# A hybrid attention and recurrence layer: down and output products with tokens on the partitions, normalised there and turned back by transposes

## The chip, the cores and the metric

The kernel runs on one NeuronCore of a Trainium2 chip. Its engines are TensorE (PE in the profile; its weight loads are PEld), VectorE (DVE), ScalarE (ACT), GpSimd (POOL) and SyncE (SP), which run their own instruction queues in order and wait for each other by semaphores. The metric is device time of one execution, in microseconds (us); less is better.

## The reference

One decoder layer on x of 512 tokens by 1024 features, all in float32:

```python
f = swiglu(rms_norm(h, ffn1_norm_pre), w_gate, w_up, w_down)      # D_FF = 2816
h = h + 0.5 * rms_norm(f, ffn1_norm_post)
u = rms_norm(h, mix_norm_pre)
q, k, v, xr, yr, gl = split(u @ w_in)                             # 3 x 1536, 2 x 1024, 2 x 1024
attn_d = dilated_attention(q, k, v) @ w_attn_branch               # 3 groups of 4 heads of 128
rec_d = (rg_lru(conv(xr)) * gelu(yr)) @ w_rec_branch
merged = sigmoid(gl[0]) * attn_d + sigmoid(gl[1]) * rec_d
h = h + rms_norm(merged @ w_out, mix_norm_post)
f = swiglu(rms_norm(h, ffn2_norm_pre), ...)                       # as the first, own weights
h = h + 0.5 * rms_norm(f, ffn2_norm_post)
```

with `swiglu(x) = (silu(x @ w_gate) * (x @ w_up)) @ w_down` and `rms_norm(x, g) = x * rsqrt(mean(x * x) + 1e-6) * g`, the mean over the 1024 features of a token.

## The kernel before

Activations lie with features on the 128 partitions and the 512 tokens along the free dimension, as eight tiles of 128 features. Every operand of a large product is split in two parts, a rounded copy and the remainder (`split`, L254: ScalarE copies, VectorE subtracts), and a product is three matrix products of the parts (`mm3`, L267). Weights come as one stream of 1 MB groups through two `raw` buffers (`raw_of`, SP's queue), are split into `w8` (four buffers of 1024 columns) or `w4` (three of 512) tiles, and are the stationary operand of `gemm` (L283); activations are the moving one, 512 or 256 tokens wide.

The gate and up products of most feed-forward tiles, and the query, key and gate products of the mixer, are made two at a time by `seven` (L518): the 2 x 2 blocks of weights (two halves of the features by two outputs) and of activations (features by two halves of 256 tokens) are multiplied with seven block products in place of eight. `w_forms` (L499) sums and splits the weights of one such group, one group ahead; `x_forms` (L420) makes the seven forms of the activations once per stage, with sums on VectorE.

The order of one feed-forward part is written out in `ffn_order` (L46): five tiles of 128 hidden features by plain products (`std`), the others by `seven` (`prod`), and between them the down products of the hidden tiles that are ready, in five parts (`FF_PARTS`), one of eight output tiles m of 128 features at a time, spread over the groups. The down sums stay in `facc`. The last part's down products are `last_product` (L371), which the output product of the mixer also uses: the last four output tiles (all eight in the second feed-forward part) are made 256 tokens wide, each is squared on ScalarE and added on VectorE (`sq_add`), and the sum over features is one product by a matrix of ones (`rstd`, L322), as features lie on partitions. Then `residual` adds to h, `pre_norm` makes the next stage's two parts with the gain alone, and the row of reciprocal roots (`r`, one per token) is multiplied onto the products later (`std_out`, `conv`, `branch`, or as `rcol` in `values`), or before the forms are made (`scaled` in `x_forms`). h is written to DRAM after each stage (`kept_m`, `kept`) and loaded again for the next residual, by POOL's queue.

A tile scheduler orders each engine's instructions by their place in the program and by priorities: weights are fetched 100 places ahead (`AHEAD`), evacuations of `seven` 200 (`EVAC`). TensorE's accumulators are five `acc` and three `aux` banks. The stage stretches that the tables use are, from the timeline: feed-forward 1 to 355, values to 423, attention and its gates to 621, attention branch and recurrence to about 833, output product to 890, feed-forward 2 to the end.

Of the kernel before, what the change touches and what calls it, by code (L numbers as in the profile page):

```python
# [10 lines left out]
F32 = mybir.dt.float32  # L11
# [5 lines left out]
P = 128  # L17
T = 512
# [4 lines left out]
NSTD = 5  # L23
NEARLY = 4
# [11 lines left out]
QKB = 7  # L36
CB = 7
# [8 lines left out]
def ffn_order():  # L46

    order = [("std", f) for f in range(NSTD)]  # L50
    order += [("prep", NSTD), ("down", 0, tuple(range(NEARLY)))]
    for a, (f0, f1) in enumerate(FF_PARTS):
        fs = range(max(f0, NSTD), f1)
        m0 = NEARLY if a == 1 else 0
# [9 lines left out]
def down_width(a):  # L64
    return (FF_PARTS[a][1] - FF_PARTS[a][0]) * P


def stream_plan():

    plan = []  # L70

    def ffn(n):
        for ev in ffn_order():
            if ev[0] == "std":
                plan.append((("gate", n, ev[1]), 1024))
                plan.append((("up", n, ev[1]), 1024))
            elif ev[0] == "prep":
                plan.append((("gu", n, ev[1]), 2048))
            else:
                for m in ev[-1]:  # L80
                    plan.append((("down", n, ev[-2], m), down_width(ev[-2])))
        for m in range(KC):
            plan.append((("down", n, len(FF_PARTS) - 1, m), down_width(len(FF_PARTS) - 1)))
# [35 lines left out]
    for m in range(KC):  # L119
        plan.append((("out", m), 1024))  # L120
# [19 lines left out]
for _n, _w in (("g1a", 8), ("g1b", 8), ("gma", 8), ("gmb", 8), ("g2a", 8), ("g2b", 8),  # L140
               ("cw", 32), ("cb", 8), ("bx", 8), ("ba", 8), ("ap", 8)):
    SMALL[_n] = (_o, _w)
    _o += _w
# [5 lines left out]
def hybrid_layer(ctx: ExitStack, tc: tile.TileContext, xT: bass.AP, wst: bass.AP, small: bass.AP,  # L149
                 consts: bass.AP, bias: bass.AP, out: bass.AP):  # L150
# [16 lines left out]
    ghalf = cpool.tile([P, 16], F32, name="ghalf")  # L167
# [9 lines left out]
    def hpair(m, sl):  # L177
        return hs["t"][m // 4][:, m % 4:m % 4 + 2, sl]
# [36 lines left out]
    def fetch(key, slot=None):  # L215

        with tc.high_priority(offset=AHEAD if slot is None else 0):
# [9 lines left out]
    def w4():  # L227
        return wpool.tile([P, 2, 512], F32R, name="w4", tag="w4", bufs=3)
# [60 lines left out]
    def gemm_first(keys, x, slots=None):  # L289
# [3 lines left out]
        for sl in HALVES:  # L293
            for k in range(x.n):
                for wt, ps in zip(wts, pss):
                    mm3(ps[:, sl], k128(wt[0])[:, k, :], k128(wt[1])[:, k, :], x.hi[k][:, sl],
                        x.lo[k][:, sl], k == 0, k == x.n - 1)
        return pss
# [11 lines left out]
    def sq_add(acc, src, sl, first, apart=False):  # L310

        for s in halves(sl):
            if first:
                ACT.activation(acc[:, s], src(s), AF.Square)
            else:
                q = ntile("sq", 2)
                ACT.activation(q, src(s), AF.Square)
                if apart:
                    return q
                DVE.tensor_add(acc[:, s], acc[:, s], q)  # L320

    def rstd(acc, r, sl, extra=None):  # L322
        for s in halves(sl):
            ps = aux_ps()[:, :HB]
            PE.matmul(ps, ones, acc[:, s], start=True, stop=extra is None)
            if extra is not None:
                PE.matmul(ps, ones, extra, start=False, stop=True)
            v, y = ntile("v", 2), ntile("y", 2)
            ACT.activation(y, ps, AF.Abs_reciprocal_sqrt, bias=eps, scale=1.0 / D)
            DVE.scalar_tensor_tensor(v, ps, D * EPS, y, op0=ALU.add, op1=ALU.mult)  # L330
            DVE.scalar_tensor_tensor(v, v, -0.5 / D, y, op0=ALU.mult, op1=ALU.mult)
            DVE.scalar_tensor_tensor(r[:, s], v, 1.5, y, op0=ALU.add, op1=ALU.mult)
# [12 lines left out]
    def pre_rstd(acc, r, sl):  # L345
        for m in range(KC):
            sq_add(acc, lambda s: hm(m, s), sl, m == 0)
        rstd(acc, r, sl)

    def gain(gi, m):  # L350
        return ghalf[:, gi * 8 + m:gi * 8 + m + 1] if gi is not None else col("gmb", m)

    def residual_end(rp, sl):

        rq = ntile("rq", 1)
        ACT.activation(rq, rp[:, sl], AF.Copy)
        t = tpool.tile([P, 2, HB], F32, name="res", tag="t")
        nc.gpsimd.tensor_mul(t, facc[:, 6:8, sl], rq[:, None, :].to_broadcast([P, 2, HB]))
        nc.gpsimd.tensor_add(hpair(6, sl), hpair(6, sl), t)
        for m in (0, 2, 4):  # L360
            t = acc_ps().rearrange("q (m t) -> q m t", m=2)
            DVE.tensor_mul(t, facc[:, m:m + 2, sl], rp[:, None, sl].to_broadcast([P, 2, HB]))
            DVE.tensor_add(hpair(m, sl), t, hpair(m, sl))

    def residual(rp, m, sl):

        t = tpool.tile([P, 2, HB], F32, name="res", tag="t")
        DVE.tensor_mul(t, facc[:, m:m + 2, sl], rp[:, None, sl].to_broadcast([P, 2, HB]))
        DVE.tensor_add(hpair(m, sl), hpair(m, sl), t)

    def last_product(key, x, evac, gi, nxt, then, slots, end=False):  # L371


        acc = npool.tile([P, T], F32, name="acc", tag="acc", bufs=2)
        rp = npool.tile([P, T], F32, name="rp", tag="r", bufs=2)
        nl = 8 if end else 4
        tails = {}
        for m in range(KC - nl):
            ps = acc_ps()
            gemm(ps, fetch(key(m)), x)  # L380
            evac(m, ps, FULL)
            sq_add(acc, lambda s: facc[:, m, s], FULL, m == 0)
            ACT.activation(facc[:, m, :], facc[:, m, :], AF.Copy, scale=gain(gi, m))
        if nl < 8:
            warm(acc)
        wts = [fetch(key(m), None if m < 4 else slots.pop(0)) for m in range(KC - nl, KC)]
        for sl in HALVES:
            for m in range(KC - nl, KC):
                ps = acc_ps()[:, :HB]
                gemm(ps, wts[m - KC + nl], x, sl)  # L390
                evac(m, ps, sl)
                last = sq_add(acc, lambda s: facc[:, m, s], sl, m == 0, end and m == KC - 1)
                ACT.activation(facc[:, m, sl], facc[:, m, sl], AF.Copy, scale=gain(gi, m))
                tails[sl.start] = last
                if m == KC - nl and sl.start:
                    rstd(acc, rp, HALVES[0], tails[0])
        for sl in HALVES:
            if sl.start:
                if end:
                    rp = acc_ps()  # L400
                rstd(acc, rp, sl, tails[HB])
            if end and sl.start:
                residual_end(rp, sl)
            for m in range(KC):
                if m % 2 == 0 and not (end and sl.start):
                    residual(rp, m, sl)
                nxt(sl, m)
        if then:
            for sl in HALVES:
                then(sl)  # L410
# [791 lines left out]
```

## Time and profile before

| | us |
|---|---|
| median of 3 runs (lowest, highest) | 1257.12 (1255.87, 1258.87) |
| the profiled execution | 1255.59 |
| its span, first to last instruction | 1253.8 |
| TensorE busy | 1237.8 |
| VectorE busy | 965.2 |
| ScalarE busy | 706.0 |
| moved by DMA, whole span | 135.67 MB |

The profile is of one execution. Busy time is time with at least one instruction on the engine; TensorE's products overlap, so it is busy also while it goes slower than it could, and the step from one product's start to the next tells more than the durations. The clock that TensorE was granted is 0.998 of full speed over the span. In the profile's tables a line number is that of the kernel's source; where a helper issues the instruction it is the helper's line.

### The profile page before, as it was taken

Reading aid. Unit: us, or ns where it says so; the run is one execution under the profiler, and the core shown is the slowest. Engines: PE = TensorE matmul, PEld = TensorE weight load, DVE = VectorE, ACT = ScalarE, POOL = GpSimd, SP = SyncE. Lnnn points to the kernel's source line nnn. Section 1 sums busy time; section 2 is a strip of 40 time slices with the busy share of each in tenths; the row PEclk is TensorE's granted clock in tenths of the full one; section 3 lists DMA queues with packets and bytes.
Section 4 is the critical chain, followed back from the end, with each engine's and each line's share of the span. In section 5 each row is a group of like instructions: output and inputs, shape, how many; then the busy total and the mean of one; then the engine's idle time right before and its main releaser. Section 6 shows DMA issues by size and latency. Waiting matters only on the chain.

```text
span 1253.8 us, 19539 instructions
## 1 busy us (share of the span) xinstructions
PE 1237.8 (99%) x7952; PEld 1128.7 (90%) x7952; DVE 965.2 (77%) x1547; ACT 706.0 (56%) x1184; POOL 22.6 (2%) x44
## 2 busy tenths in 40 slices
PE   9999999999999999999999999999999999999996
PEld 7889999999888999999988888889988999999996
DVE  7987777787588788889676987753998777777755
ACT  6555444454565565566636879536655544445543
POOL 0000000000002000000100000000000000000000
PEclk9999999999999999999999999999999999999999
DMA  6223333333515232221442231323222222223232
GB/s 241 70 90 102 106 105 104 105 113 129 207 73 167 89 110 77 75 103 68 135 139 96 77 126 67 135 85 117 101 102 93 93 101 102 101 102 118 102 135 68
DMA packets 26811, 135.67 MB, mean 108 GB/s; under 512 B 3297, under 2 KB 5473, under 8 KB 14561
## 3 DMA queue, kind: packets, MB, share of 16 engines
q1 hardware_dynamic: 24064, 122.88, 28.1%
q0 software_dynamic: 2656, 11.54, 2.7%
q8 instruction: 62, 1.02, 0.3%
q14 instruction: 29, 0.23, 0.1%
HBM read 127.07 MB, written 6.29 MB: 106 GB/s over the span
## 4 chain that ended last, share of the span: by engine, by line
PE 87%; DVE 8%; ACT 2%; DMA 1%; issue 1%; SPq 0%; DVEq 0%
PE acc L269 13%; PE acc L268 13%; PE acc L270 13%; PE acc L527 11%; PE acc L528 11%; PE acc L529 11%; PE aux L529 2%; PE aux L528 2%; PE aux L527 2%; DVE w L256 2%; PE acc L736 1%; PE acc L735 1%; PE acc L734 1%; DMA raw<-in_w 1%; DVE acc L320 1%
## 5 line engine op out<-in xcount | busy, mean ns | idle before, releaser
L256 DVE TENSOR_TENSOR w<-raw,w 128x1024 fp32r<-128x1024 f32 (+2 forms) x307 | 302.0, 989 | 110.0 <-ACT w L255 109.7
L255 ACT ACTIVATE w<-raw 128x1024 fp32r<-128x1024 f32 (+2 forms) x307 | 262.5, 867 | 190.5 <-PE aux L529 55.1
L528 PE MATMUL acc<-big,w 128*128 128x256 f32 x928 | 263.4, 284 | 0.0
L527 PE MATMUL acc<-big,w 128*128 128x256 f32 x928 | 263.3, 284 | 0.0
L529 PE MATMUL acc<-big,w 128*128 128x256 f32 x928 | 263.1, 284 | 0.0
L269 PE MATMUL acc<-act,w 128*128 128x512 f32 (+1 forms) x524 | 191.5, 366 | 1.2 <-DVE act L256 0.8
L270 PE MATMUL acc<-act,w 128*128 128x512 f32 (+1 forms) x524 | 191.2, 365 | 0.8 <-DVE w L256 0.8
L268 PE MATMUL acc<-act,w 128*128 128x512 f32 (+1 forms) x524 | 191.4, 367 | 0.0
L527 PEld LDWEIGHTS acc<-big,w 128*128 128x128 f32 x928 | 177.8, 192 | 1.8 <-ACT c L534 0.4
L528 PEld LDWEIGHTS acc<-big,w 128*128 128x128 f32 x928 | 177.8, 192 | 1.4
L529 PEld LDWEIGHTS acc<-big,w 128*128 128x128 f32 x928 | 177.9, 192 | 0.0
L534 ACT ACTIVATE c<-acc 128x256 f32<-128x256 f32 x166 | 63.4, 382 | 98.5 <-PE acc L529 92.5
L270 PEld LDWEIGHTS acc<-act,w 128*128 128x128 f32 x524 | 98.9, 189 | 17.5 <-DVE w L256 1.7
L269 PEld LDWEIGHTS acc<-act,w 128*128 128x128 f32 x524 | 99.0, 189 | 16.6 <-DVE act L256 1.9
L268 PEld LDWEIGHTS acc<-act,w 128*128 128x128 f32 x524 | 98.8, 189 | 15.8 <-ACT act L341 0.6
L268 PE MATMUL acc<-big,w 128*128 128x512 f32 (+1 forms) x240 | 91.7, 382 | 0.0
L270 PE MATMUL acc<-big,w 128*128 128x512 f32 (+1 forms) x240 | 91.7, 382 | 0.0
L269 PE MATMUL acc<-big,w 128*128 128x512 f32 (+1 forms) x240 | 91.7, 382 | 0.0
L528 PE MATMUL aux<-big,w 128*128 128x256 f32 x272 | 77.0, 283 | 0.0
L529 PE MATMUL aux<-big,w 128*128 128x256 f32 x272 | 77.0, 283 | 0.0
L527 PE MATMUL aux<-big,w 128*128 128x256 f32 x272 | 77.0, 283 | 0.0
L256 DVE TENSOR_TENSOR w<-s,w 128x1024 fp32r<-128x1024 f32 x50 | 61.1, 1221 | 4.9 <-ACT w L255 4.9
(278 smaller groups left out, 2411.4 us busy)
## 6 DMA issues: line engine op xcount, KB each, us to landing
raw<-in_w SPq DMA_DIRECT2D x89, 1024.0 KB, 4.9
raw<-in_w SPq DMA_DIRECT2D x23, 512.0 KB, 3.7
raw<-in_w SPq DMA_DIRECT2D x6, 768.0 KB, 4.2
raw<-in_w SPq DMA_DIRECT2D x16, 256.0 KB, 3.0
raw<-in_w SPq DMA_DIRECT2D x3, 896.0 KB, 4.7
h<-in_x SPq DMA_DIRECT2D x8, 256.0 KB, 5.4
h<-in_x POOLq DMA_DIRECT2D x8, 256.0 KB, 5.3
kept_m<-h POOLq DMA_DIRECT2D x2, 1024.0 KB, 4.5
```

Of the source, the lines that this page charges most:

```text
L255: ACT.activation(dh, src, AF.Copy)
L256: DVE.tensor_sub(dl, src, dh.bitcast(F32))
L268: PE.matmul(ps, wh, xh, start=first, stop=False)
L269: PE.matmul(ps, wh, xl, start=False, stop=False)
L270: PE.matmul(ps, wl, xh, start=False, stop=last)
L320: DVE.tensor_add(acc[:, s], acc[:, s], q)
L527: PE.matmul(ps, wh, xh, start=start and k == 0, stop=False, skip_group_check=True)
L528: PE.matmul(ps, wh, xl, start=False, stop=False, skip_group_check=True)
L529: PE.matmul(ps, wl, xh, start=False, stop=k == 3, skip_group_check=True)
L534: ACT.activation(c, ps, AF.Copy)
L734: PE.matmul(pss[b], um.hi[k][:, bl], wh[:, i, :], start=k == 0, stop=False)
L735: PE.matmul(pss[b], um.hi[k][:, bl], wl[:, i, :], start=False, stop=False)
```

## The change

The down products and the output product exchange their operands: 128 tokens of activations are stationary and 512 columns of weights move, so a result has tokens on the partitions, four blocks b of 128 tokens by two halves of 512 features. `facc` and h take that layout (`fb`, `hb`), x is loaded once more in it (`xN`) for the residual, and the output is written in it. A token's mean square is then a sum along the free dimension: `square` takes it as ScalarE's accumulator, and `root` works on columns of 128 x 1. Gains of the norms are rows that a POOL load repeats on all partitions (`gains`).

`Boundary.block` ends a block of tokens: reciprocal root, residual, copy to DRAM, the root of the new h, and u, the normalised input with its gain. `Boundary.turn` transposes u back to features on partitions and makes the two parts of the next input from it, and a plain copy into `facc`. As u is normalised already, the row `r` falls away after feed-forward 1's input; std_out, values, conv and the gates read their products as they are. The same `u` is kept through attention and recurrence; before, its parts were made a second time after attention.

Of the seven forms, three are now the parts themselves; the mixer uses them in place, feed-forward 2 copies them by six POOL transfers. Down products come in halves of 48 products, through two own weight buffers `wd`, in place of output tiles of 12. Feed-forward 2 makes four tiles by plain products in place of five. Pools of `qk`, `c` and `w4` tiles have one buffer less.

```diff
-NSTD = 5
+NSTD = {1: 5, 2: 4}
@@ ffn_order
-    order += [("prep", NSTD), ("down", 0, tuple(range(NEARLY)))]
+    order += [("prep", NSTD[n]), ("down", 0, 0)]
...
-            n, k = len(fs), KC - m0
-            ms = range(m0 - (-k * i // n), m0 - (-k * (i + 1) // n))
-            order.append(("prod", f, a - 1, tuple(ms)))
+            c, k = len(fs), len(halves)
+            order.append(("prod", f, a - 1, halves[i * k // c:(i + 1) * k // c]))
@@
+    def root(sums, f):
+        with tc.high_priority(offset=EVAC):
+            tot, y, v, r = (stat() for _ in range(4))
+            DVE.tensor_add(tot, sums[0], sums[1])
+            ACT.activation(y, tot, AF.Abs_reciprocal_sqrt, bias=eps, scale=1.0 / D)
+            refine(r, v, y, tot, f)
+        return r
+
+    def square(src):
+        q, t = tmp("sq"), stat()
+        ACT.activation(q, src, AF.Square, accum_out=t)
+        return t
+
+    def tokens(ps, ws, x, b, fill=lambda: None):
+        bl = slice(b * P, (b + 1) * P)
+        for k in range(x.n):
+            wh, wl = (w.rearrange("p (k c) -> p k c", k=2)[:, k % 2, :] for w in ws[k // 2])
+            PE.matmul(ps, x.hi[k][:, bl], wh, start=k == 0, stop=False)
+            PE.matmul(ps, x.hi[k][:, bl], wl, start=False, stop=False)
+            PE.matmul(ps, x.lo[k][:, bl], wh, start=False, stop=k == x.n - 1)
+            if k == x.n // 2 - 1:
+                fill()
...
+    def last_product(key, nk, x, added, grow, slots, block, fills={}):
+        sums = {}
+        warm(eps)
+        for half, fs in enumerate(FHALVES):
+            ws = [fetch(key(half, kk), slots.pop(0) if half else None) for kk in range(nk)]
+            for b in range(4):
+                ps = acc_ps()
+                tokens(ps, ws, x, b, fills.get((half, b), lambda: None))
+                src, y = ps, fb(b, fs)
+                if added:
+                    DVE.tensor_add(y, ps, y)
+                    src = y
+                sums[b, half] = square(src)
+                DVE.tensor_mul(y, src, grow[:, fs])
+                if half:
+                    block(b, (sums[b, 0], sums[b, 1]))
+
+    class Boundary:
...
+        def block(self, b, sums):
+            r = root(sums, self.f)
+            DVE.scalar_tensor_tensor(hb(b), fb(b), r, hb(b), op0=ALU.mult, op1=ALU.add)
+            nc.gpsimd.dma_start(self.kept[b], hb(b))
+            r = root([square(hb(b, fs)) for fs in FHALVES], 1.0)
+            us = []
+            for fs in FHALVES:
+                u = tmp("u")
+                DVE.scalar_tensor_tensor(u, hb(b, fs), r, self.grow[:, fs], op0=ALU.mult, op1=ALU.mult)
+                us.append(u)
+            self.u[b] = us
+
+        def turn(self, b):
+            for i, u in enumerate(self.u.pop(b)):
+                ps = aux_ps()
+                for j in range(4):
+                    PE.transpose(ps[:, j * P:(j + 1) * P], u[:, j * P:(j + 1) * P], ident)
+                src = ps.rearrange("p (k t) -> p k t", k=4)
+                hi, lo = (t[:, :, b * P:(b + 1) * P] for t in (self.his[i], self.los[i]))
+                ACT.activation(hi, src, AF.Copy)
+                DVE.tensor_sub(lo, src, hi.bitcast(F32))
+                ACT.activation(fb(b, FHALVES[i]), ps, AF.Copy)
...
+        def copies():
+            for name in ("p1", "p2", "p3"):
+                v = big([P, 2, 4, HB])
+                for i in range(2):
+                    nc.gpsimd.dma_start(v[:, i], t[name][i])
+                t[name] = v[:, 0], v[:, 1]
...
+    def block1(b, sums):
+        bd1.block(b, sums)
+        if b >= 2:
+            bd1.turn(b - 2)
+
+    last_product(*end1, True, grow1, spare(ap1), block1)
@@ values, first group
-                for bs in ((0, 1), (2, 3)):
+                for b in range(4):
                     for kk in range(4):
-                        part(kk, bs)
-                roots()
+                        part(kk, (b,))
+                    if b < 2:
+                        bd1.turn(b + 2)
...
+    last_product(lambda half, kk: ("out", half, kk), 4, mg, False, grow3, slots, bd2.block,
+                 {(1, 3): lambda: (bd2.turn(0), bd2.turn(1))})
+    keys = [(w, 2, i) for i in range(NSTD[2]) for w in ("gate", "up")]
+    pss = gemm_first(keys[:NFIRST], u2, [spare(ap2)[2]],
+                     {3: [lambda: bd2.turn(2)], 4: [lambda: bd2.turn(3)]})
...
+    def block2(b, sums):
+        r = root(sums, 0.5)
+        for fs in FHALVES:
+            DVE.scalar_tensor_tensor(hb(b, fs), fb(b, fs), r, hb(b, fs), op0=ALU.mult, op1=ALU.add)
+            nc.sync.dma_start(out[b][:, fs], hb(b, fs))
```

More of the change, by code (lines that the diff above doesn't have):

```diff
@@ L365, in residual @@
[L365 to L410, printed above, removed]
@@ L435, in form_t2 @@
-        def form_t2():
-            form("p6", d[2], pool.tile([P, 2, 4, HB], F32R, name="tx", tag="tx"))
+            v = tile_ if tile_ is not None else big([P, 2, 4, HB])
+            t[name] = v[:, 0], v[:, 1]
+            split(v[:, 0], v[:, 1], src)
         def sum1():
```

365 lines of the change are left out of this document (181 added, 184 removed).

## The prediction

> **What bounds the kernel now.** I read the page's busy times and its chain first, then TensorE's timeline in the middle of a feed-forward block, then the stage table, and last the end of VectorE's timeline. The page:
>
> ```profile
> PE 1237.8 (99%) x7952; PEld 1128.7 (90%) x7952; DVE 965.2 (77%) x1547; ACT 706.0 (56%) x1184; POOL 22.6 (2%) x44
> ...
> PE 87%; DVE 8%; ACT 2%; DMA 1%; issue 1%; SPq 0%; DVEq 0%
> ```
>
> TensorE is hardly ever idle and holds 87% of the chain, so the time is a count of matrix products times their spacing, plus what TensorE waits where stages meet, plus head and tail. The spacing is read from start to start, not from the durations, which overlap:
>
> ```profile
> 305.47 0.28 PE L528 MATMUL aux<-big,w 128*128 128x256 f32 x1
> 305.59 0.28 PE L529 MATMUL aux<-big,w 128*128 128x256 f32 x1
> ...
> 305.71 0.40 PE L268 MATMUL acc<-act,w 128*128 128x512 f32 x1
> 305.95 0.40 PE L269 MATMUL acc<-act,w 128*128 128x512 f32 x1
> 306.18 0.39 PE L270 MATMUL acc<-act,w 128*128 128x512 f32 x1
> ```
>
> A product 256 wide takes 0.120 us, one 512 wide 0.227 us (the median over all of them; single steps here read 0.23 and 0.24). The stage table (columns: stretch; length; busy us and records of PE, PEld, DVE, ACT, POOL; clock; DMA) says where the other engines press:
>
> ```profile
> 338.00:424.00 86.00, 85.95 (x450) 73.43 (x450) 70.07 (x116) 50.78 (x90) 8.95 (x18) 1.00 0.34 116
> 665.00:775.00 110.00, 108.78 (x478) 89.10 (x477) 90.94 (x119) 87.97 (x113) 0.00 (x0) 1.00 0.27 96
> 833.00:959.00 126.00, 124.85 (x756) 111.44 (x755) 95.73 (x151) 72.65 (x128) 1.09 (x2) 1.00 0.29 105
> 959.00:1205.00 246.00, 246.00 (x1749) 232.35 (x1748) 185.49 (x281) 123.60 (x202) 1.06 (x2) 1.00 0.33 113
> ```
>
> PE busy hides small waits, so I counted the timeline. From 862.46 to 958.43 (second half of the output product, start of feed-forward 2) there are 444 products 256 wide (53.3 us), 168 of 512 (38.1) and 8 fp32 records of the row sums (0.215 each, 1.7): 93.1 us of work in 95.97, so 2.9 us waited. From 338.05 to 423.46 (end of feed-forward 1, values) the same count leaves 0.6. The tail:
>
> ```profile
> 1241.75 0.42 DVE L618 TENSOR_TENSOR facc<-acc,facc 128x256 f32<-128x256 f32 x1 [0.83 <-PE acc L270]
> 1243.92 0.42 DVE L330 SCALAR_TENSOR_TENSOR v<-aux,y 128x256 f32<-128x256 f32 x1 [1.75 <-ACT y L329]
> 1245.72 1.29 DVE L362 TENSOR_TENSOR acc<-facc,acc 128x512 f32<-128x512 f32 x2 [0.45 <-ACT rq L356]
> 1248.84 0.69 DVE L363 TENSOR_TENSOR h<-acc,h 128x512 f32<-128x512 f32 x1
> ```
>
> The last product's slot ends at 1241.55 and the span at 1253.8: 12.3 us of tail, 4.3 of them after VectorE's last instruction (output transfer and end).
>
> **The change part by part.** The profiled execution took 1255.59 us (span 1253.8), 1.5 under the median of 1257.12; differences are worked on the span and laid on the median.
>
> *TensorE's own work.* (a) 624 products of half width (144 in feed-forward 1's last product, 192 in the output product, 288 in feed-forward 2's) become 312 of full width with activations stationary: 624 x 0.120 = 74.9 against 312 x 0.227 = 70.8, -4.1. That form is in the trace already (values, L734 to L736) at the same 0.227. By the Trainium skill, TensorE: Matmul & The Clock Gate, section Back-to-back issue gap, a warm isolated product takes N/2.4 + 2.5 ns, 109 and 216; (a) would then be worth an estimated 0.8 and the forecast 1252.6. The trace's 120 and 227 disagree with it, so I take the trace and give the rule no chance. (b) Tile 4 of feed-forward 2 goes from two plain products (48 x 0.227 = 10.9) to the seven-product form (84 x 0.120 = 10.1): -0.8. (c) Ten row-sum products by ones before the last product's end, 0.43 each by two records: -4.3; four transposes of roots: -0.4. (d) 64 transposes, at 0.44 per four by the chain's rows of L879: +7.0. Sum -2.6.
>
> *Waits that go.* At 324.7 (0.31) and 1207.4 (0.95) TensorE waits for the last activation tile to be split, with only one or two small down products (2.7 us each) as cover. After, a whole down half (48 x 0.227 = 10.9) stands there: -1.3. What is late next is the first gain row, whose load waits for that half's weight buffer: VectorE waits for it, and TensorE has five accumulators, 20 us at 4.1 us per token block, against 5.3 us for a POOL load. Cost nothing.
>
> *The two boundaries.* The order of the changed kernel as built says what TensorE does meanwhile. After feed-forward 1 each token block ends a chain on VectorE and ScalarE: sum 0.69, square 0.66 plus reading the accumulator 0.1, root 1.09 (one-column instructions at 0.20 start to start as L861 and L862, a reciprocal root at 0.29 as the warm-up on L336), residual over 1024 columns 1.28, two squares 1.32, root 1.09, two gain products 1.35, eight handovers at 0.03: 7.8 us. While it waits, VectorE also does the next block's sum and gain (1.2) and the turned block's two subtractions (1.2). Between one block's transposes and the next's TensorE has 28 to 30 products and eight transposes: 7.3 to 7.7 us. If the next block's first two steps overlap, the chains come every 7.3 to 7.9 us; laid out in the built order I get waits of about 0.3 at each turn: 1.1 in place of 0.6. In the output product blocks come every 5.5 us and the first feed-forward products are interleaved by halves of the contraction; I find 0.6 at the second half of block 1 (its copy stands behind two weight splits and two squares in ScalarE's queue) and 0.9 at the last turn: 1.5 in place of 2.9. Bounds: nothing, where the other work in the gaps is ready; and full serial chains, 7.8 + 2.4 = 10.2 per block against 7.3, three turns: 9, and 6 at the output product, whose blocks are further apart. I take 1.1 + 1.5, nearest the overlapped layout, since VectorE in 833 to 959 shows 76% busy with such interleaving. Net -0.9.
>
> A reciprocal-root table load (1.283 in the trace) now starts each boundary's first chain; in the trace the next activation follows at once (load at 677.98, next at 679.27), so it is in the layout at 1.3. The Trainium skill, ScalarE: Activation LUTs, section What ACT_TABLE_LOAD costs, adds about 1.38 us of drain to each load. No row here shows it.
>
> *Forms.* Three of seven input forms are no longer split in the mixer and feed-forward 2, and scaling and re-normalising go: VectorE and ScalarE lose work where VectorE was busy 70 of 86 us; TensorE did not wait there, so nothing. Feed-forward 2 copies its three forms by six POOL transfers of 512 KB. The nearest row, h<-kept of 1024 KB, lands in 6.2 us; six in a row 37, and they are needed after the second half of the first products, three more and a down half (14.4 + 16.3 + 10.9 = 41.6). Nothing, with 4 to spare for the first form and 10 more for the third; copies that cost nothing and copies 5 us late are the ends. The rest of POOL's queue: residual inputs as three times four loads of 512 KB for 8 + 8 of 256 and 2 of 1024, kept copies as 4 + 4 writes for 2 + 2, five gain rows; at the second boundary each write waits for its block and the form copies stand behind it, then the reload of the residual, needed some 270 us later. SP's queue moves the same weight bytes in fewer loads and eight output transfers as before. One buffer less for small weights, query/key tiles and product copies: each is read within the group that follows, so nothing; if that cover fails it shows as a wait within a run, priced below.
>
> *Runs of products.* Down halves now stand together (10.9 us) and leave runs of three or four seven-product groups, 10.1 us each, without cover. Per group VectorE issues four sums of weights (0.60 start to start), three splits (1.14), one small (0.60), four of 256 (0.35), two of 512 (0.60): 9.0 us, 89%; waits for ScalarE are extra. In the attention stage three groups stand together with 7.8 and TensorE loses nothing. One group of weights is ready ahead, 10 us of slack, so +0.5; bounds 0 and 6 (four splits at 0.36 each, VectorE's wait for ScalarE of 110.0 us over the 307 splits of L256, make it 10.4 per group, 0.3 too long, over some 19 groups in runs).
>
> *Recurrent stage.* VectorE loses the row products by the root; ScalarE gets eight strided copies (0.63; VectorE's strided twin took 1.01) and is busy 88 of 110 us. TensorE waits 1.7 there now. I take 0, bounds -1.7 and +2.
>
> *Tail.* Last slot to VectorE 0.2, sum 0.72, square 0.78, add 0.23, own gain ahead of the root's last three 0.6, those 0.6, two residual halves 1.35, end 4.3: 8.8 for 12.3, -3.5. Bounds -4 and -2.5.
>
> Sum: -2.6 - 1.3 + 0.5 - 1.4 + 0.5 + 0 - 3.5 = -7.8: **1249.3 us**.
>
> **Rivals.**
> 1. *The block chains do not overlap* (slower). Place: VectorE and ScalarE at the two boundaries, where one in-order queue carries sums, roots and subtractions of three blocks. Price: 15 in place of 2.6, +12.4: 1262. It decides from 12.9 us of boundary waits, a chain spacing of about 9. For it: VectorE must wait for ScalarE five times per block. Against: those waits are where the other blocks' work stands. Chance 0.10.
> 2. *VectorE falls behind in the runs*: +5.5, 1255. For: 89% load. Against: 246 us at 75% busy without a wait. 0.13.
> 3. *No boundary waits and a freer recurrent stage*: -2.6 and -1.7, 1245. For: VectorE loses eight products at 1.01 and eight at 0.69 there. Against: ScalarE at 80%. 0.16.
> 4. *Each table load stalls ScalarE once more for its own length*: 1.3 at each boundary, 1252. Against: the 0.01 us after the load above. 0.04. By the Trainium skill's drain (the page and section above) it would be an estimated 2.8 in all, 1252.1.
>
> **How the numbers follow.** The forecast holds 0.55, with its own range 1246.5 to 1252.5; 0.02 is left for something slower that I do not name. A measurement of this kernel cannot tell less than about 0.2% (2.5 us) from no change. Faster: 0.55 + 0.16 + 0.04 and a third of rival 2 = 0.80; same: the rest of it, 0.08; slower: 0.10 + 0.02 = 0.12. The range takes in rivals 2 to 4 and their spread, not rival 1: 1244 to 1258.
>
> **What would show it.** Right: TensorE's 256-wide records about 550 fewer and 512-wide 264 more; waits at the eight turns under 0.6 each; the span ending about 9 us after the last product; TensorE starts unbroken through the runs. Wrong: TensorE waiting for u (the normalised block) at the transposes by more than 1.5 each, or for weight splits inside the runs, or the form copies landing after the first group of feed-forward 2 begins.

## The result, and the profile after

The changed kernel takes 1250.45 us, the median of five runs (1248.69 to 1251.04), against 1257.12 for the kernel before: a ratio of 0.9946, 95% interval 0.9932 to 0.9961, or 6.7 us less. The forecast was 1249.3, 7.8 us less. The profiled execution of after took 1251.04 us, the slowest of its five, with a span of 1249.3; against the span of before, 1253.8, it shows 4.5 of the 6.7 us. The rest is the choice of executions: that of before was 1.5 below its median, that of after 0.6 above its own.

The page of after, its busy times and its chain by engine:

```profile
PE 1235.0 (99%) x7712; PEld 1117.5 (89%) x7712; DVE 911.3 (73%) x1427; ACT 670.5 (54%) x1105; POOL 26.1 (2%) x51
...
PE 90%; DVE 5%; ACT 4%; DMA 1%; issue 1%; SPq 0%; DVEq 0%; ACTq 0%
```

VectorE has 54 us less work and ScalarE 35 less, and little of that is in the time (the end, below, is the exception): TensorE is still busy 99% and holds 90% of the chain. So I count TensorE's timeline as the prediction did: every product at its own spacing (0.227 for 512 wide, 0.120 for 256, 0.111 for 128 by 128, 0.215 for a record of a row sum), and whatever a step takes beyond that is lost. Between the two profiles:

| us | before | after | difference | forecast |
|---|---|---|---|---|
| TensorE's products at their spacing | 1223.3 | 1221.0 | -2.3 | -2.6 |
| first product begins at | 5.6 | 6.2 | +0.6 | 0 |
| lost up to 20 us | 1.0 | 1.9 | +1.0 | 0 |
| lost from 20 to 320 (runs of feed-forward 1) | 0.9 | 0.5 | -0.4 | with the runs of 2: +0.5 |
| lost at the last tile's split, 324.7 and 1207.4 | 1.6 | 0 | -1.6 | -1.3 |
| lost at boundary 1 | 0.5 | 1.3 | +0.8 | +0.5 |
| lost in attention | 3.7 | 4.0 | +0.2 | 0 |
| lost in the recurrent stage | 2.0 | 4.3 | +2.4 | 0 |
| lost at boundary 2 | 3.1 | 0.7 | -2.4 | -1.4 |
| lost from 1000 to 1200 (runs of feed-forward 2) | 0.2 | 0.8 | +0.6 | see above |
| last product's slot to the end | 12.3 | 8.7 | -3.6 | -3.5 |

(The row of the last tile's split holds all that is lost from 320 to 338 and from 1200 to the last product. In the row of attention 2.3 is no wait, in both kernels: 24 fp32 products of the scores step by 0.215 and are counted at 0.120. The rows are rounded, and their sums miss the spans by up to 0.4.) The products are as forecast: 4552 records of 256 wide for 5116, 2808 of 512 wide for 2544. One step stands out against the forecast, the recurrent stage. TensorE's waits in the profile of after, what it waited for:

```profile
PE aux L276 <- ACT gt L1060: 3.2, 4, 1.5
PE aux L719 <- DVE eps L197: 1.1, 1, 1.1
PE acc L276 <- ACT act L353: 0.5, 1, 0.5
PE aux L439 <- DVE u L431: 0.5, 2, 0.2
```

The first row, four waits of 3.2 us in all, is the recurrent stage: a gate product (L276) waits for a bank that the sigmoid (L1060) must read first. The last row is what the prediction feared most, the turns (L439) waiting for a normalised block: 0.5 in all. At the first boundary the four turns begin here (start, duration, engine, what):

```profile
351.55 0.66 PE L439 MATMUL aux<-cst,u 128*128 128x128 f32 x4
...
359.53 0.66 PE L439 MATMUL aux<-cst,u 128*128 128x128 f32 x4
...
367.32 0.63 PE L439 MATMUL aux<-cst,u 128*128 128x128 f32 x4 [0.24 <-DVE u L431]
...
375.02 0.63 PE L439 MATMUL aux<-cst,u 128*128 128x128 f32 x4 [0.23 <-DVE u L431]
```

They are 8.0, 7.8 and 7.7 apart; the prediction had chains "every 7.3 to 7.9". In feed-forward 2 four groups and nothing else stand from 949.4 to 989.6. The first and the second of them (stretch; length; busy us and records of PE, PEld, DVE, ACT, POOL; clock; DMA):

```profile
949.40:959.45 10.05, 10.05 (x85) 10.05 (x84) 3.67 (x6) 5.20 (x8) 0.00 (x0) 1.00 0.05 8
959.45:969.50 10.05, 10.05 (x86) 10.05 (x85) 9.21 (x15) 6.13 (x10) 0.00 (x0) 1.00 0.32 108
```

Over all four VectorE is busy 31.8 of 40.2 us, 7.9 per group, but that mean hides two kinds of group: in the first VectorE has been idle for 7.9 us when it gets its first result at 952.54, and in the second (and in the third, with the same 9.21) it is busy 92%. So the prediction's 9.0 per group is about right, and TensorE starts without a break all the same. The end, VectorE and the last product:

```profile
1230.08 1.28 ACT L366 ACT_TABLE_LOAD   x1
...
1240.36 0.39 PE L382 MATMUL acc<-big,act 128*128 128x512 f32 x1
1240.54 1.42 DVE L1138 SCALAR_TENSOR_TENSOR h<-facc,stat,h 128x512 f32<-128x512 f32 x2
1241.87 0.69 DVE L408 TENSOR_TENSOR facc<-acc,facc 128x512 f32<-128x512 f32 x1
...
1244.66 1.42 DVE L1138 SCALAR_TENSOR_TENSOR h<-facc,stat,h 128x512 f32<-128x512 f32 x2
```

The last block's sum (L408) does not follow the last product but the previous block's two residual halves (L1138): VectorE comes late to the last block.

### The profile page after: what moved, and what is told of

Same layout as the page of the kernel before. It is cut to its first block, busy times and chain, and to the rows that moved or that the text cites. A ratio compares the mean times of both kernels' runs of the same rounds, so it can differ in the third digit from the quotient of the medians.

```text
span 1249.3 us, 18949 instructions
## 1 busy us (share of the span) xinstructions
PE 1235.0 (99%) x7712; PEld 1117.5 (89%) x7712; DVE 911.3 (73%) x1427; ACT 670.5 (54%) x1105; POOL 26.1 (2%) x51
## 4 chain that ended last, share of the span: by engine, by line
PE 90%; DVE 5%; ACT 4%; DMA 1%; issue 1%; SPq 0%; DVEq 0%; ACTq 0%
PE acc L585 11%; PE acc L586 11%; PE acc L587 11%; PE acc L381 7%; PE acc L382 7%; PE acc L380 7%; PE acc L276 7%; PE acc L278 7%; PE acc L277 7%; PE aux L585 3%; PE aux L586 3%; PE aux L587 3%; PE acc L784 1%; PE acc L786 1%; PE acc L785 1%; DVE w L264 1%
## 5 line engine op out<-in xcount | busy, mean ns | idle before, releaser
L264 DVE TENSOR_TENSOR w<-raw,w 128x1024 fp32r<-128x1024 f32 (+1 forms) x241 | 257.9, 1074 | 115.8 <-ACT w L263 84.8
L263 ACT ACTIVATE w<-raw 128x1024 fp32r<-128x1024 f32 (+1 forms) x241 | 225.3, 938 | 181.5 <-DVE raw L566 60.4
L585 PE MATMUL acc<-big,w 128*128 128x256 f32 x880 | 251.2, 285 | 0.1
L586 PE MATMUL acc<-big,w 128*128 128x256 f32 x880 | 250.2, 284 | 0.0
L587 PE MATMUL acc<-big,w 128*128 128x256 f32 x880 | 249.9, 284 | 0.0
L585 PEld LDWEIGHTS acc<-big,w 128*128 128x128 f32 x880 | 168.7, 192 | 1.2 <-ACT c L592 0.3
L586 PEld LDWEIGHTS acc<-big,w 128*128 128x128 f32 x880 | 168.9, 192 | 0.6
L587 PEld LDWEIGHTS acc<-big,w 128*128 128x128 f32 x880 | 168.8, 192 | 0.0
L380 PE MATMUL acc<-wd,act 128*128 128x512 f32 x256 | 99.9, 390 | 0.0
L381 PE MATMUL acc<-wd,act 128*128 128x512 f32 x256 | 99.9, 390 | 0.0
L382 PE MATMUL acc<-wd,act 128*128 128x512 f32 x256 | 99.5, 390 | 0.0
L585 PE MATMUL aux<-big,w 128*128 128x256 f32 x280 | 79.4, 283 | 0.0
L586 PE MATMUL aux<-big,w 128*128 128x256 f32 x280 | 79.3, 283 | 0.0
L587 PE MATMUL aux<-big,w 128*128 128x256 f32 x280 | 79.3, 283 | 0.0
L585 PE MATMUL acc<-tx,w 128*128 128x256 f32 x268 | 76.2, 284 | 0.0
L586 PE MATMUL acc<-tx,w 128*128 128x256 f32 x268 | 76.0, 283 | 0.0
L587 PE MATMUL acc<-tx,w 128*128 128x256 f32 x268 | 75.9, 283 | 0.0
L276 PE MATMUL acc<-big,w 128*128 128x512 f32 x192 | 74.8, 389 | 0.0
L278 PE MATMUL acc<-big,w 128*128 128x512 f32 x192 | 74.8, 389 | 0.0
L277 PE MATMUL acc<-big,w 128*128 128x512 f32 x192 | 74.8, 389 | 0.0
L264 DVE TENSOR_TENSOR w<-s,w 128x1024 fp32r<-128x1024 f32 x51 | 62.4, 1224 | 10.4 <-ACT w L263 10.3
```

The costliest lines, as they stand in the source:

```text
L263: ACT.activation(dh, src, AF.Copy)
L264: DVE.tensor_sub(dl, src, dh.bitcast(F32))
L276: PE.matmul(ps, wh, xh, start=first, stop=False)
L277: PE.matmul(ps, wh, xl, start=False, stop=False)
L278: PE.matmul(ps, wl, xh, start=False, stop=last)
L380: PE.matmul(ps, x.hi[k][:, bl], wh, start=k == 0, stop=False)
```

## The experiments

Each ratio is to the kernel before, timed beside the edit on the same chip; of the second profile of before there is a single execution.

### The changed kernel again, and the start

No edit.

> The changed kernel once more, unaltered, as the base of this call. In its first profile the first eight products of TensorE came 0.43 us apart until 10.2, where the kernel before went at 0.23 from 6.6, because the load of sm landed later and TensorE stood 0.5 us between its warm-up and the first product; this put 1.6 us on that one execution. Theory A: the landing of sm varies from run to run, so this execution may start either way, and the ratio to before stays between 0.9932 and 0.9961. Theory B: the change itself makes the load late (more loads on the queues at the start); then the slow start is here again, in this run and in all that follow.

1249.33 us (ratio 0.9940, 0.9928 to 0.9953), 7.9 below the kernel before on its chip, span 1247.9. TensorE's first products, in after and then here:

```profile
6.20 2.08 PE L276 MATMUL acc<-act,w 128*128 128x512 f32 x4 [0.52 <-ACT act L353]
8.07 0.63 PE L277 MATMUL acc<-act,w 128*128 128x512 f32 x1
8.50 0.63 PE L278 MATMUL acc<-act,w 128*128 128x512 f32 x1
```

```profile
6.67 1.21 PE L276 MATMUL acc<-act,w 128*128 128x512 f32 x4 [1.48 <-ACT act L353]
7.71 0.40 PE L277 MATMUL acc<-act,w 128*128 128x512 f32 x1
7.95 0.39 PE L278 MATMUL acc<-act,w 128*128 128x512 f32 x1
```

The gap ahead of the first product is longer here (1.48), and yet the products step by 0.24 and not 0.43: nothing is lost but the gap. So the start varies, and the gap is not what sets the rate. The warm-ups were lengthened, and the kernel before was profiled once more:

```diff
-WARM = 10
+WARM = 14
```

> Fourteen warm-up products at the start in place of ten (two records each, 0.21 us). In three of five profiles of the changed kernel and its variants the first eight products of TensorE ran 0.43 apart until about 10 us; in all five TensorE stood 0.5 to 1.5 us between the last warm-up and the first product, as sm landed 3.8 to 4.2 us after its issue (3.0 in the profile of before). Theory: the slow start comes from that gap; with the warm-ups lasting until about 6.5 the first products run at 0.227 in every execution: -1.6 us where the start was slow, +0.3 where it was not, so the median falls by 0.5 to 1. Rival: the clock rises after a fixed time whatever TensorE does, and the median does not move.

> The kernel before, unaltered, for one more look at its start. Theory A: sm lands about 3.0 us after its issue again and TensorE goes from its warm-up to the first product within 0.3 us at full spacing; the late load is then of the change's making. Theory B: its landing varies by run, and a start like that of the changed kernel is seen here too.

With 14 warm-ups the median is 1250.49: no gain (ratio 0.9942, 0.9930 to 0.9955), though its own profile had no gap. In the second profile of before sm landed 3.0 us after its issue, as in the first, but in that of an edit on before (the bank run, below) after 4.0 with a gap of 0.8; in those of the changed kernel and its edits it landed after 2.6 to 4.2. This supports theory A of the first expectation: the landing varies by run. The second profile of before, taken alone, fits its theory A, but the edit on before, with its late landing, bears out theory B. The slow start, eight or nine products at 0.43 until about 10.2, stands in three of the eleven profiles of the changed kernel and edits on it, and in none of the three of before and an edit on it; that is too few to say that the change has no part in it. Set against the other profiles, it cost the profiled execution of after some 1.6 us; without it that execution would have stood near 1249.4, within the range of its kernel.

### TensorE's own work: width and transposes

```diff
-                tokens(ps, ws, x, b, fills.get((half, b), lambda: None))
+                tokens(ps, ws, x, b, fills.get((half, b), lambda: None), HALVES)
```

Here `tokens` goes over the two halves of 256 columns in turn.

> The three last products (feed-forward 1, output, feed-forward 2) are made 256 columns wide again, with activations stationary as in the changed kernel: 312 products of 512 become 624 of 256. By the trace's spacing (0.120 and 0.227 us from start to start): 624 x 0.120 - 312 x 0.227 = +4.1 us against the unaltered kernel of this call. Rival: the spacing is not what the time follows, since TensorE waits at the boundaries anyway and the extra time is taken out of those waits (1.4 us at the first boundary, 0.7 at the second): +2. By the Trainium skill, TensorE: Matmul & The Clock Gate, section Back-to-back issue gap, an isolated product takes N/2.4 + 2.5 ns and the difference would be an estimated +0.8.

1254.70 us (ratio 0.9981, 0.9972 to 0.9990), 5.4 above the unaltered kernel on the same chip. The expectation miscounted: the edit halves both halves of the three products, 480 of 512 wide, where the kernel before had only 624 of 256 wide in them. By the spacing that is 960 x 0.120 - 480 x 0.227 = +6.2. The steps of these products and of the down halves, which share their lines, add up to 290.2 us for 284.0 in the unaltered run, +6.2; as much is lost at the boundaries, within 0.2, and 0.7 less behind the last product, as VectorE is then less late. The spacing is what the time follows, and the rival that the waits absorb it is out. The formula that the Trainium skill, TensorE: Matmul & The Clock Gate, section Back-to-back issue gap, gives for an isolated product would make it an estimated 480 x 2.5 ns = +1.2, and the measurement disagrees with that.

```diff
-                for j in range(4):
+                for j in range(8):
+                    j %= 4
                     PE.transpose(ps[:, j * P:(j + 1) * P], u[:, j * P:(j + 1) * P], ident)
```

> Each of the 64 transposes that turn the normalised blocks back is issued twice in a row into the same place: 64 more at 0.11 us. Theory: they stand on TensorE's path, +7.0 us, all of it at the two boundaries; at the first boundary, where block chains and turns follow each other in a closed loop, the turns move about 0.4 to 0.8 further apart than the 7.7 to 8.0 us of the changed kernel. Rival: TensorE would have waited there for the next block in any case, and the waits take up most of it: less than +3.

1256.48 us (ratio 0.9992, 0.9984 to 1.0001): +7.15 against +7.0 expected, so 64 transposes more cost their full 7 us, and those of the change, of the same kind and in the same places, are taken to cost as much. The detail on the turns was wrong: they moved to 8.4, 7.25 and 7.2 apart, two of the three closer together, as the order around them was built anew: 22 products stand between these, for 28.

### The recurrent stage, the step that failed

The timeline of after at the first gate set of the stage, ScalarE and the waiting product:

```profile
678.64 1.08 ACT L1027 ACTIVATE xr<-acc 128x512 f32<-128x512 f32 x1
...
679.52 1.07 ACT L263 ACTIVATE w<-raw 128x1024 fp32r<-128x1024 f32 x1
...
680.48 0.80 ACT L1029 ACTIVATE sig<-xr,sm 128x512 f32<-128x512 f32 x1
...
681.30 1.28 ACT L1060 ACT_TABLE_LOAD   x1
...
682.59 1.84 ACT L1060 ACTIVATE gt<-aux,sm 128x512 f32<-128x512 f32 x3
...
683.33 0.50 PE L276 MATMUL aux<-rec,w 128*128 128x512 f32 x1 [0.75 <-ACT gt L1060]
```

ScalarE goes without a pause from the strided copy (L1027, 1.08 us) through a weight split and the table load to the first sigmoid, and the fourth gate product waits for the bank that this one reads. Two edits, each alone:

```diff
-                    ACT.activation(ip(xr[:, 3:]), pi(ps), AF.Copy)
+                    DVE.tensor_copy(ip(xr[:, 3:]), pi(ps))
```

> In the recurrent stage the strided copy of the convolution input out of the accumulator goes back from ScalarE to VectorE, the engine that made it in the kernel before (there as a product by the row of roots). ScalarE's copy takes 1.08 us, twice per head ahead of the table load and the sigmoids that free TensorE's banks. Theory: these 2.2 us per head make TensorE wait there, 4.3 us in the changed kernel against 2.0 before; with them on VectorE the waits fall to about 2.0, so -2.3 us. Rival: VectorE is the later engine of that chain (its three tap products, 2.3 us, follow the copy), and the waits stay: 0 within 0.5.

1247.19 us (ratio 0.9921, 0.9907 to 0.9934), 2.1 below the unaltered kernel on the same chip; the stage loses 2.2 in place of 4.3, as the theory had it.

```diff
-                    ps = aux_ps()
+                    ps = aux_ps() if w or j == 0 else acc_ps()
```

> The changed kernel, with one edit in the recurrent stage: the fourth gate product of each head takes one of the five acc banks in place of one of the three aux banks. TensorE waits there for an aux bank that the first sigmoid (ScalarE, after the strided copies and a table load) has to free: 4.3 us in the changed kernel. Theory A: the wait is for the bank alone, and with a fourth bank it goes: TensorE loses under 1 us in the stage, -3.5 us. Theory B: the gates are late as a chain, and what follows them (accumulators that wait for ScalarE) waits in their place: a gain under 1.

1244.78 us (ratio 0.9902, 0.9888 to 0.9915). All of TensorE's waits in this profile:

```profile
PE aux L719 <- DVE eps L197: 1.1, 1, 1.1
PE aux L439 <- DVE u L431: 0.5, 2, 0.3
```

The waits for the sigmoid are gone, nothing took their place, and the stage loses nothing. It was the bank: theory A. This kernel is faster than both: 12.6 us below the kernel before on its chip, and about 5 below the changed one. The same edit on the kernel before:

> The kernel before with the same one edit as in the gate-bank run: the fourth gate product of each head takes an acc bank. The kernel before loses 2.0 us to three waits for an aux bank in the recurrent stage. Theory: they go, -2.0 us (about 1255.4); the changed kernel lost 4.4 there, so of its gain from this edit 2.4 undoes what the strided copies on ScalarE had cost, and 2.0 was there before. Rival: without the copies on ScalarE the bank is not what ends these waits, and nothing changes.

1255.00 us (ratio 0.9991, 0.9982 to 1.0000). The stage loses nothing here either, 2.0 less. The median fell by 1.5, and the profile shows a wait for a weight split at the last product (1206.5, [1.21 <-ACT act L255] in its line) that was 0.5 in one profile of before and absent in the other. So by the timelines 2.0 of the 4.4 that the bank gives the changed kernel were there before, and 2.4 undo what the change did.

### The boundaries and the end

```diff
-            refine(r, v, y, tot, f)
+            for _ in range(2):
+                refine(r, v, y, tot, f)
```

> The three one-column instructions that refine each root are issued twice, with the same result: 0.6 us more per root on VectorE, two roots per block at a boundary, one per block at the end. Theory: at the first boundary the chains run in a closed loop with the turns (a block's chain starts only when VectorE has made the turned block before it), so each of its four turns comes 1.2 later, +4.8; the second boundary, where TensorE waits 0.7 in all, has slack of its own and gives 0 to +2.4; the end +0.6: together +5.4 to +7.8. Rival: the chains of neighbouring blocks overlap, as the prediction's layout had it, and only the first one's length is paid once at each place: +1.2 and +0.6, about +2.

1261.58 us (ratio 1.0029, 1.0018 to 1.0041): about 11 above the changed kernel, more than the theory's 5.4 to 7.8 and far from the rival's 2. TensorE's turns at the first boundary:

```profile
351.49 0.66 PE L440 MATMUL aux<-cst,u 128*128 128x128 f32 x4 [0.21 <-DVE u L432]
...
360.92 1.38 PE L440 MATMUL aux<-cst,u 128*128 128x128 f32 x8 [1.02 <-DVE u L432]
...
369.88 1.29 PE L440 MATMUL aux<-cst,u 128*128 128x128 f32 x8 [1.61 <-DVE u L432]
...
378.77 1.29 PE L440 MATMUL aux<-cst,u 128*128 128x128 f32 x8 [1.54 <-DVE u L432]
```

They are 9.4, 9.0 and 8.9 apart, 1.2 to 1.5 more than before the edit, which is about the 1.2 added to each chain: one block's chain ends (in after with u, at 352.2) before the next one's root begins (at 352.7), and every us of it is a us at every turn. The rest over the forecast is in three places. The first boundary lost 8.7 for 1.3, of which some 1.8 are not waiting at all: behind the last wait nine products step by 0.43 or near it. The stretch table of this kernel (here the clock is the last column but two):

```profile
379.00:384.00 5.00, 4.94 (x18) 3.45 (x17) 2.80 (x4) 3.64 (x7) 2.65 (x6) 0.66 0.37 96
```

The second boundary lost 4.5 for 0.7, more than the 2.4 allowed for it, and the end grew by 1.3, twice the added root. So a chain that is 1.2 us longer per block turns the gain into a loss: the prediction's first rival, which was to decide from 12.9 us of boundary waits and a chain spacing of about 9, was that near (13.2 are lost here).

The table load ahead of the first root was then moved off the chain. The dummy roots that should have done this read a constant, and the scheduler had put all of them at the start of the kernel:

```diff
-        warm(eps)
         for half, fs in enumerate(FHALVES):
...
+            if not half:
+                warm(sums[3, 0])
```

> The changed kernel, with the dummy reciprocal root that last_product issues ahead of its blocks made to read a sum of squares of the first half (it reads a constant now, and the scheduler put all three at the very start). The table load of 1.28 us then stands before the first root of each boundary and of the end, not in its chain. Theory: VectorE and ScalarE go from block to block in a chain that has no slack, so a delay of the first block is carried to the last: at the end, where the last block's sum starts 1.28 after the last product's start in place of about 0.4, the span ends 1.0 earlier; at the first boundary the waits at the turns fall from 1.4 to 0.2 to 0.6. Together -1.5 to -2.2. Rival: the chains' own length sets both places (turns 7.7 apart against 7.3 of TensorE's work, blocks 4.12 apart at the end against 4.08), and an earlier start is lost again within three blocks: -0.3.

1248.92 us (ratio 0.9946, 0.9933 to 0.9958). The end:

```profile
1225.00 1.28 ACT L348 ACT_TABLE_LOAD   x1
...
1239.37 0.39 PE L382 MATMUL acc<-big,act 128*128 128x512 f32 x1
1239.79 0.69 DVE L407 TENSOR_TENSOR facc<-acc,facc 128x512 f32<-128x512 f32 x1
```

The last sum follows the last product by 0.42, and the end takes 7.6 for 8.7: the theory was right there. At the first boundary nothing changed (1.4 lost): there the rival was right, the chain's own length sets the turns and an earlier start is lost again. The profile lost 1.3 elsewhere, at 63 to 66, for the split of the fourth plain tile, after a start that was 1.2 earlier than in the unaltered run (whether the one follows from the other is not shown); the median is 0.4 to 1.5 below those of the changed kernel.

Last, the chain was cut in two, with the late dummy root and the bank edit in the same kernel:

```diff
-            r = root([square(hb(b, fs)) for fs in FHALVES], 1.0)
-            us = []
+            self.sq[b] = [square(hb(b, fs)) for fs in FHALVES]
+            if b:
+                self.scale(b - 1)
+            if b == 3:
+                self.scale(3)
+
+        def scale(self, b):
+            r = root(self.sq.pop(b), 1.0)
+            us = []
```

> Three edits on the changed kernel: the fourth gate product in an acc bank, the dummy root late (both as run alone), and a boundary's block cut in two: the second root and the normalised rows of block b are issued after the first half of block b + 1. Theory: the turns of the first boundary are 7.7 to 8.0 apart because one block's chain ends before the next one's root begins; with the two halves beside each other the spacing falls to TensorE's own 7.3, and the waits at these turns from 1.4 to under 0.5. With 4.4 from the bank and 1.1 from the end: -6.5 against the changed kernel, about 1243.5. Rival: VectorE takes its queue in order, so the later second half makes the turned blocks later by as much as it saves: waits at the turns of 1.4 or more, about 1245.

1250.57 us (ratio 0.9951, 0.9939 to 0.9964). The bank and the end kept what they had given (0 lost in the stage, 7.5 at the end), but the first boundary lost 3.4 and the second 5.3. TensorE's waits at the turns and for the parts made from u:

```profile
PE aux L447 <- DVE u L439: 1.3, 3, 0.6
PE acc L276 <- ACT act L450: 1.1, 1, 1.1
...
PE acc L277 <- DVE act L451: 0.9, 1, 0.9
...
PE acc L792 <- ACT big L450: 0.7, 1, 0.7
```

The rival was right and its price too small: in an in-order queue the second half stands behind the next block's first half, so u comes later, and the parts that are made from it (L450, L451) with it. Not all of the 5.3 is that: behind these waits the granted clock fell to 0.50 for 3.41 us, as with the longer roots, and some 1.5 went there:

```profile
891.65:895.06 3.41, 3.41 (x18) 3.41 (x18) 1.85 (x6) 1.58 (x6) 0.00 (x0) 0.50 0.92 329
```

### VectorE in the runs

```diff
-            DVE.tensor_add(s12[:, 0, :], s12[:, 1, :], g0)
+            for _ in range(5 if key[0] == "gu" else 1):
+                DVE.tensor_add(s12[:, 0, :], s12[:, 1, :], g0)
```

> In both feed-forward parts one sum of weights per seven-product group is issued five times in place of once, with the same result: 4 x 0.6 = 2.4 us more of VectorE per group, over 35 groups 84 us. Theory: in the stretch of four groups and nothing else from 949 VectorE was busy 31.8 of 40.2 us, 7.9 per group and not the 9.0 of the prediction; with 2.4 more it is 10.3 against TensorE's 10.05, and the down halves (10.9 us with 5 to 6 of VectorE) take up the rest: 0 to +1.5. Rival: as the prediction's second rival had it, VectorE's waits for ScalarE bring it to 10.4 per group without the sums; with them 12.8, four groups and two halves need 63 us or more against 62 of TensorE, and the first groups of a run wait: +6 to +12.

1250.30 us (ratio 0.9955, 0.9943 to 0.9968), no different from the changed kernel (1250.45 and 1249.33). Its page:

```profile
PE 1233.3 (99%) x7712; PEld 1115.8 (89%) x7712; DVE 991.2 (79%) x1567; ACT 669.9 (54%) x1105; POOL 26.1 (2%) x51
```

80 us more of VectorE cost under 1.5: one wait of 0.9 at 938, and 0.4 more from 1000 to 1200. So the second rival is out, but not because VectorE has room. The expectation's 10.3 us per group rests on the mean of 7.9; the groups within a run have 9.2, with the added sums an estimated 11.6, and in this run's profile VectorE is busy 9.9 and 10.0 of 10.05 us in the second and third group of the same stretch. It falls behind there, and TensorE does not notice within the run. That the group of weights that is ready ahead covers it, as the prediction had it, is the likely reason; no run took that slack away.

## Why the prediction was right, point by point

- TensorE's own work: -2.6 forecast, -2.3 in the timeline, and the width and the transposes each measured alone: 6.2 by count and 6.2 in the steps of the timeline, 7.0 by count and 7.15 in the median.
- The waits at the last tile's split, forecast to go, went.
- Boundary 1: 1.3 lost where 1.1 was forecast, for the reason given. The added roots showed how little slack that was.
- Boundary 2: 0.7 lost where 1.5 was forecast; the two waits of 0.6 and 0.9 that the layout found were not there. That the work between the blocks covers their chains held; where it would not cover them was wrong, by 0.8.
- Runs: the two rows of the table together +0.2 for +0.5. VectorE's load per group, 9.0 by start-to-start steps, was about right (9.2 busy within a run), and so was the small price put on it: 2.4 more per group cost under 1.5 in all.
- The form copies: the last was issued at 913.5 and the slowest of the six took 9.1 us, so they had landed by 923, for a first group at 949.4. The 4 us to spare were 26, as the copies began when their own blocks were turned and not after the last.
- The end: 8.8 forecast, 8.7 measured, which is luck, by two errors that cancel. The last sum begins 1.5 after the last product's start, or 1.3 after its slot, and not 0.2, because the table load (which the prediction put into the boundaries' chains but not into the end's) made VectorE late by 1.1, as the late dummy root showed. And what follows VectorE's last instruction takes 3.2 and not 4.3.
- The recurrent stage is the step that failed: "I take 0, bounds -1.7 and +2", and the runs show +2.4, outside its own bounds. The term that was mis-sized is the strided copy, priced at ScalarE's 0.63 with VectorE's 1.01 for the same pattern standing beside it; it takes 1.08 on ScalarE, twice per head, in the chain ahead of the sigmoids. Moved back, 2.1 us return; whether a copy of 0.63 would have cost nothing there, no run shows. With the copy on VectorE the kernel is 10 us below the kernel before on its chip, where the unaltered one is 7.9 below; the forecast was 7.8.
- That the total came out within 1.1 us is luck in part: the +2.4 of the recurrent stage stand against 0.8 less lost than forecast at boundary 2, 0.3 less in the runs and 0.3 less at the last tile's split.
- The third rival (no boundary waits and a freer recurrent stage) had its second half the wrong way round. The fourth, a second stall at each table load, was not seen: in after ScalarE's next activation stands at 682.59 behind the load at 681.30. By the Trainium skill, ScalarE: Activation LUTs, section What ACT_TABLE_LOAD costs, a drain of about 1.38 us comes on top; no row here shows it.

## What to carry to other kernels

Price a moved copy by its access pattern, from the nearest row with the same pattern on any engine, and ask what stands behind it on the engine that it moves to: here a table load and the instruction that frees the bank TensorE wants. A wait for a bank can be cheaper to remove by another bank (4.4 us here) than by relieving the engine that frees it (2.1); the timeline shows it when the waiting product names the reader of an older result. Where blocks go one by one through an in-order queue, the chain's length counts at every block and an earlier start counts only at the last; lengthen it by a seventh, as here, before trusting that it is hidden. A mean load over a stretch can hide a first group in which an engine had nothing to do: read it group by group.

## What the runs showed of the hardware that was not expected

- TensorE's rate fell by half after waits, twice. In the kernel with longer roots the waits at three turns were 1.0, 1.6 and 1.5 us, and behind the last of them nine products of 512 stepped by 0.43 or near it, with the granted clock 0.66 over 379 to 384. In the kernel with the chain cut in two it was 0.50 over 891.65 to 895.06, behind waits of 1.1 and 0.9 at the second boundary. Both falls lasted 3.41 us, and in the 3.41 us ahead of each TensorE's products covered 1.8. The first cost some 1.8 us and the second 1.5, beside the waits themselves. At 366.75 of the kernel with longer roots the same 1.8 of 3.41 were covered and no fall came, so what decides is not shown.
- At the start the half rate ended at 4.2 to 6.4 us in eleven profiles, with gaps of 0 to 1.5 us ahead of the first product, and only at 10.1 to 10.3 in three, with gaps of 0.5 to 0.9. The Trainium skill, TensorE: Matmul & The Clock Gate, section What's actually happening, says that the clock is set by a free-running window of about 3.4 us, so that the moment of the rise depends on where the window falls. The traces agree on the window: in all fourteen, the time from the first rise of the granted clock to its fall behind the last product is a whole multiple of 3.413 us (in after 1235.6, 362 times). The latest rise is 6.1 us behind the earliest, more than one window can explain, and why the clock did not rise one window earlier in the three stays open.
